# A decoder layer on one core: the norm before the last gate split into weights and sigmoid, and separate homes for the down projection's sums and one load buffer

## The chip, the cores and the metric

The kernel runs on one core of one Trainium2 chip. The metric is the device time of one execution in microseconds (us), lower is better. The core has five engines with instruction queues of their own that run in parallel and wait for each other by semaphores: TensorE (PE; its weight loads are listed as PEld), VectorE (DVE), ScalarE (ACT), GpSimd (POOL) and SyncE (SP). Each engine takes its instructions strictly in the order in which they were written to its queue, so a waiting instruction holds up all that stand behind it. SP and POOL also issue the DMA transfers.

## What is computed

One decoder layer on 512 tokens of width 1024, in float32. The parts that matter here are the last three: the down projection of the MLP, its norm, and the gated input embedding.

```
ff = (gelu(u_gate) * u_val) @ w_down            # (512, 2816) @ (2816, 1024)
x = x + rmsnorm(ff, mlp_post_norm)
e = p @ w_ple                                    # (512, 256) @ (256, 1024)
out = x + sigmoid(rmsnorm(x, ple_norm) @ w_ple_gate) * e
rmsnorm(t, g) = t * rsqrt(mean(t * t, -1) + 1e-6) * g
```

## The kernel before, in words

**Precision.** Every matrix is kept as a pair hi + lo: ACT copies the float32 source to a rounded type (`hi`, L72), DVE subtracts (`lo`, L73). `mm3` (L56 is its helper) makes one product out of three matmuls: hi*hi, hi*lo, lo*hi. A weight arrives by `chunk` (L137): a DMA into a raw buffer, then this split.

**Buffers.** SBUF is handed out by pools that open and close like a stack on each side. Raw buffers come from rings: `W["rings"]["raw"]` is `rawp` (2) + `rawb` (1), and for the first half of the down projection the pool `rx` adds 2 more, so 5. `rx` is opened after `close_qp()`, on the memory that the pool `qp` held. `qp` holds the tiles `X` and `f2h` of the up projection, from which POOL writes each pair's sums to DRAM (`dd`, L797). A raw buffer of `rx` can thus be loaded only when those DMAs have read their source.

**Up projection.** For each of 22 blocks `j`, 48 matmuls into two PSUM banks `pu`; ACT and DVE do the convolution and GELU (`conv_gelu`, L814 to L822), and after every second block `ff_sums` (L785 to L797) makes sums of token blocks.

**Down projection.** It is Strassen's scheme with seven products on 2x2 blocks, over 11 chunks `c`. The first half takes for each chunk two raw tiles of `w_down` (`r1`, 512 KB, L888; `r2`, 256 KB, L889), makes their sums and differences on DVE (L893 to L895), and runs 24 matmuls into the eight banks `M1`, `M5`, `M7`, `M6`. `drain` (L916 to L923) then combines the banks into six tiles: `U`, `V12` and `C22`, two each. In the second half every chunk needs one raw tile more (L934) and 12 matmuls (into `M1` and `M3`); then `M4` follows with 66 matmuls whose right sides were kept in SBUF as `T2`. `T2t` are two tiles of 8 x 512 elements: `T2t[0]` and three slots of `T2t[1]` hold the `T2`, and the other five slots of `T2t[1]` hold five of the six tiles out of `drain`; the sixth is `T4v`.

**Norms and gate.** `post_norm(n, ...)` (L720) takes one block of 128 tokens: squares and their sum on ACT (L725), the power -1/2 on POOL (L728), scaling by the gain on DVE (L731), the residual add into `xn` (L732), the square of `xn` on ACT (L733), the power on POOL (L102), and the scaling by that and by the gain `g_next` on DVE (L735) into `t`. `to_hT` (L738) transposes `t` by 8 matmuls with the identity into PSUM (`ptr`, L60), and ACT and DVE split it into `hT[0]` and `hT[1]` (L747, L748). At the end `hT` is allocated anew as `h3T` on the memory of `T2t`: its lo half is on `T2t[1]`. The gate is 192 matmuls into `pg`; `finish` and `last_halves` apply the sigmoid (ACT), multiply by `e`, add `xn` (DVE) and store.

**Order.** The order of each engine's queue is set by a scheduler when the program is built, which goes by its own estimate of durations, by the priorities (`hot`) and by when buffers come free. So a change of a buffer's home moves instructions on all engines. Transfers issued by `load` (L865) are tied into one order on POOL.

Of the kernel before, what the change touches and what calls it, by code (L numbers as in the profile page):

```python
# [29 lines left out]

PP_QA, PP_KVA, PP_BG, PP_W0, PP_W1, PP_W2, PP_CB = 0, 2, 3, 19, 63, 107, 151
PP_N = 195

# [4 lines left out]
def hybrid_kernel(ctx, tc, T):  # L38
# [97 lines left out]

    def chunk(src, n=1024, parts=1, dst=None):  # L137
        raw = wtile("raw" if not W["slots"] or (W["raw"] + W["lo"]) & 2 == 0 else "lo", F32)
        w = n // parts
        for i in range(parts):  # L140
            nc.sync.dma_start(raw[:, i * w:(i + 1) * w], src[:, i * w:(i + 1) * w])
        hi = dst[0] if dst else wtile("hi", F32R)
        if dst:
            lo = dst[1]
        elif W["slots"]:
            lo = W["slots"].pop(0)
            W["slots"].append(lo)
        else:
            lo = wtile("lo", F32R)
        if parts == 1:  # L150
            split(hi[:, :n], lo[:, :n], raw[:, :n])
        else:
            for i in range(parts):
                u = slice(i * w, (i + 1) * w)
                dve.tensor_copy(hi[:, u], raw[:, u])
                dve.tensor_tensor(lo[:, u], raw[:, u], f32(hi[:, u]), ALU.subtract)
        return hi, lo
# [495 lines left out]

    def loadgain(src, go=nc.sync.dma_start):
        t = res["bcp"].tile([P, D], F32, name="gain", tag="gain", bufs=2)
        go(t, src.partition_broadcast(P))
        return t
# [61 lines left out]

    def post_norm(n, ps, gp, gn):  # L720
        xn = res["xn"]
# [135 lines left out]
    close_qp()  # L857
    vp, close_vp = opened(name="vp", bufs=1, side="right")
    rx, close_rx = opened(name="rx", bufs=1, side="right")
    R2 = W["rings"]["raw"]  # L860
    W["rings"]["raw"] = R2 + [(rx, 2)]

# [41 lines left out]

    T4v = vp.tile([P, S], F32, name="T4v")
    close_rx()
    W["rings"]["raw"] = R2
    open_res()
    xn = res["xn"]
    g_post, g_next = loadgain(T["mlp_post"], load), loadgain(T["ple_norm"], load)  # L910
    for n in range(NB):
        load(xn[:, n, :], xd[n])
    parts = [T2t[1][:, i] for i in range(3, 8)] + [T4v]
    U, V12, C22 = (parts[2 * i:2 * i + 2] for i in range(3))

# [32 lines left out]
    for n in range(2):  # L948
        dve.tensor_tensor(V12[n], M3[n], V12[n], ALU.add)
        ts[n] = post_norm(n, (M["M1"][n], V12[n]), g_post, g_next)  # L950
    M4 = banks(2, "M4")
# [18 lines left out]
    for n in (2, 3):  # L970
        dve.tensor_tensor(U[n - 2], M4[n - 2], U[n - 2], ALU.add)
        ts[n] = post_norm(n, (U[n - 2], C22[n - 2]), g_post, g_next)


    for n in range(NB):
        b = slice(n * P, (n + 1) * P)
        for half in range(2):
            ps = bank(1 + 2 * (n % 2), "pe")
            w = slice(half * S, (half + 1) * S)
            for k in range(2):  # L980
                mm3(ps, ph[:, k, b], pl[:, k, b], wph[:, k, w], wpl[:, k, w], k == 0, k == 1)
            act.activation(e[:, n, w], ps, AF.Copy)
    hT = [hp.tile([P, 8, S], F32R, name=f"h3T{i}", tag=f"hT{i}") for i in range(2)]
    for n in range(NB):
        to_hT(n, ts[n], n // 2 * 2)
    cg = [chunk(T["wpg"][k]) for k in range(4)]
    wx = [qkp.tile([P, 4, 1024], F32R, name="wy" + t, tag=t) for t in ("kT", "qT")]
    cg += [chunk(T["wpg"][4 + k], dst=[t[:, k, :] for t in wx]) for k in range(4)]
    lB = fp.tile([P, 4, S], F32, name="lB", tag="fB")
# [15 lines left out]
    def last_halves(n, half):  # L1005
        g = [bank(n, "pg") for _ in range(2)]
        b = slice(n * P, (n + 1) * P)
        for i in range(2):
# [4 lines left out]
            o = otile()[:, :256]  # L1013
            act.activation(o, g[i][:, :256], AF.Sigmoid)
            dve.tensor_tensor(o, o, e[:, n, u], ALU.mult)
# [3 lines left out]
    def finish(n, half, pg, parts=1):  # L1019
        o = otile()  # L1020
        q = S // parts
        for i in range(parts):
            u = slice(i * q, (i + 1) * q)
            w = slice(half * S + i * q, half * S + (i + 1) * q)
            act.activation(o[:, u], pg[:, u], AF.Sigmoid)
            dve.tensor_tensor(o[:, u], o[:, u], e[:, n, w], ALU.mult)
            dve.tensor_tensor(o[:, u], o[:, u], xn[:, n, w], ALU.add)
            nc.sync.dma_start(T["out"][n * P:(n + 1) * P, w], o[:, u])

    pg = {(n, half): bank(1 + 2 * n, "pg") for n in (0, 1) for half in range(2)}  # L1030
    gate_mms(pg, (0, 1), (0, 1))
# [18 lines left out]
def layouts(i):  # L1050
# [19 lines left out]
    pp = np.concatenate([col(i["q_a_norm"][0]), col(i["kv_a_norm"][0]),  # L1070
                         col(i["b_gate"][0]), cw[0], cw[1], cw[2], cb], 1)
    q, k = np.arange(P)[:, None], np.arange(P)[None, :]
# [28 lines left out]
        "mlp_post": f(np.asarray(i["mlp_post_norm"])[0]),  # L1101
        "ple_norm": f(np.asarray(i["ple_norm"])[0]),
        "cst": f(cst),
# [33 lines left out]
```

## Time and profile before

| | us |
|---|---|
| median of 3 runs (lowest, highest) | 761.18 (760.98, 762.81) |
| the profiled execution | 759.25 |
| its span, first to last instruction | 757.5 |
| PE busy | 731.1 (97%) |
| DVE busy | 534.3 (71%) |
| ACT busy | 362.3 (48%) |
| mean granted clock of TensorE | 0.985 |

The median is 1.93 us above the profiled execution, and this is 1.75 us above its span. Busy time of PE counts a matmul until its modelled end, so "busy" is no measure of speed: when the clock is granted at half, PE is just as busy and does half the work. Idle time of an engine matters only where nothing else was due on the one that ends last; a wait is put down to the releaser that came last.

### The profile page before, as it was taken

Reading aid. Unit: us, or ns where it says so; the run is one execution under the profiler, and the core shown is the slowest. Engines: PE = TensorE matmul, PEld = TensorE weight load, DVE = VectorE, ACT = ScalarE, POOL = GpSimd, SP = SyncE. Lnnn points to the kernel's source line nnn. Section 1 sums busy time; section 2 is a strip of 40 time slices with the busy share of each in tenths; the row PEclk is TensorE's granted clock in tenths of the full one; section 3 lists DMA queues with packets and bytes.
Section 4 is the critical chain, followed back from the end, with each engine's and each line's share of the span. In section 5 each row is a group of like instructions: output and inputs, shape, how many; then the busy total and the mean of one; then the engine's idle time right before and its main releaser. Section 6 shows DMA issues by size and latency. Waiting matters only on the chain.

```text
span 757.5 us, 9555 instructions
## 1 busy us (share of the span) xinstructions
PE 731.1 (97%) x3496; PEld 605.7 (80%) x3496; DVE 534.3 (71%) x939; ACT 362.3 (48%) x634; POOL 84.3 (11%) x100
## 2 busy tenths in 40 slices
PE   9999999999999999999999999999985999999797
PEld 8988877778888778898888888888874888787686
DVE  6568788986775493849767676767657866789632
ACT  5843677755444243638444544444323443377321
POOL 0104023000000150200000000000000223001100
PEclk9999999999999999999999999999995999999999
DMA  8612221222122545514434344433314987946011
GB/s 308 244 32 63 60 84 42 66 74 71 42 84 84 192 141 167 172 52 141 144 133 138 140 138 141 133 125 110 133 55 155 318 263 238 353 132 195 0 57 56
DMA packets 30959, 99.90 MB, mean 132 GB/s; under 512 B 4128, under 2 KB 5408, under 8 KB 30912
## 3 DMA queue, kind: packets, MB, share of 16 engines
q1 hardware_dynamic: 25248, 76.75, 30.8%
q0 software_dynamic: 5664, 22.55, 8.2%
q8 instruction: 27, 0.44, 0.2%
q14 instruction: 20, 0.16, 0.1%
HBM read 85.98 MB, written 12.85 MB: 130 GB/s over the span
## 4 chain that ended last, share of the span: by engine, by line
PE 61%; issue 26%; DVE 7%; DMA 3%; ACT 1%; POOL 1%; SPq 0%; POOLq 0%; DVEq 0%
PE M L56 12%; PE psg L56 11%; PE pg L56 6%; PE yo L56 6%; PE pu L56 4%; PE puh L56 3%; PE psA L56 3%; PE psba L56 3%; PE psC L56 2%; PE psB L56 2%; PE scm L56 2%; DVE wlo L73 2%; DMA wraw<-in_wd 1%; PE pb L56 1%; POOL dd L797 1%
## 5 line engine op out<-in xcount | busy, mean ns | idle before, releaser
L56 PE MATMUL pu<-hT,whi 128*128 128x512 f32 x640 | 197.1, 389 | 0.0
L72 ACT ACTIVATE whi<-wraw 128x1024 fp32r<-128x1024 f32 (+4 forms) x109 | 106.7, 980 | 182.3 <-PE pu L56 75.3
L73 DVE TENSOR_TENSOR wlo<-wraw,whi 128x1024 fp32r<-128x1024 f32 (+2 forms) x103 | 120.5, 1173 | 69.0 <-ACT whi L72 65.5
L56 PEld LDWEIGHTS pu<-hT,whi 128*128 128x128 f32 x640 | 120.1, 188 | 24.8
L56 PE MATMUL pu<-hT,wlo 128*128 128x512 f32 x320 | 124.5, 389 | 0.0
L56 PEld LDWEIGHTS pu<-hT,wlo 128*128 128x128 f32 x320 | 60.1, 188 | 12.6
L56 PE MATMUL psg<-xh,whi 128*128 128x512 f32 x128 | 51.1, 400 | 1.3 <-DVE ga L422 0.9
L56 PE MATMUL psg<-xl,whi 128*128 128x512 f32 x128 | 50.8, 397 | 0.0
L56 PE MATMUL psg<-xh,wlo 128*128 128x512 f32 x128 | 50.8, 397 | 0.0
L814 ACT ACTIVATE cv<-pu,pp 128x512 f32<-128x512 f32 x40 | 30.6, 765 | 9.1 <-PE pu L56 9.1
L815 DVE SCALAR_TENSOR_TENSOR cv<-pu,pp,cv 128x511 f32<-128x511 f32 x40 | 29.8, 745 | 4.7 <-ACT cv L814 4.7
L72 ACT ACTIVATE whi<-T 128x512 fp32r<-128x512 f32 (+1 forms) x33 | 24.4, 766 | 17.4 <-PE M L56 12.2
L56 PE MATMUL M<-whi,ffxh 128*128 128x512 f32 x64 | 22.4, 439 | 9.3 <-ACT whi L72 9.3
L816 DVE SCALAR_TENSOR_TENSOR cv<-pu,pp,cv 128x510 f32<-128x510 f32 x40 | 29.9, 747 | 1.1
L817 ACT ACTIVATE cv<-cv 128x512 f32<-128x512 f32 x22 | 13.9, 632 | 33.6 <-DVE cv L816 33.6
L797 POOL DMA_DIRECT2D dd<-f2h x11 | 6.0, 546 | 214.9 <-ACT f2h L794 214.9
L670 POOL TENSOR_TENSOR gx<-gx,ga 128x512 f32<-128x512 f32 x8 | 14.8, 1870 | 133.3 <-DVE gx L669 133.3
L56 PEld LDWEIGHTS psg<-xh,whi 128*128 128x128 f32 x128 | 24.0, 188 | 7.0 <-DVE ga L422 1.1
L73 DVE TENSOR_TENSOR wlo<-T,whi 128x512 fp32r<-128x512 f32 (+1 forms) x33 | 27.3, 862 | 1.0 <-ACT whi L72 0.9
L56 PEld LDWEIGHTS psg<-xl,whi 128*128 128x128 f32 x128 | 24.1, 188 | 4.9 <-issue 0.2
L56 PEld LDWEIGHTS psg<-xh,wlo 128*128 128x128 f32 x128 | 24.1, 188 | 4.8
L56 PEld LDWEIGHTS M<-whi,ffxh 128*128 128x128 f32 x64 | 13.4, 214 | 13.3 <-ACT whi L72 10.5
(314 smaller groups left out, 1652.6 us busy)
## 6 DMA issues: line engine op xcount, KB each, us to landing
wraw<-in_wup SPq DMA_DIRECT2D x44, 512.0 KB, 3.4
wraw<-in_wd SPq DMA_DIRECT2D x22, 512.0 KB, 4.7
wraw<-in_wg SPq DMA_DIRECT2D x16, 512.0 KB, 3.4
dd<-f2h POOLq DMA_DIRECT2D x11, 384.0 KB, 3.0
dd<-X POOLq DMA_DIRECT2D x11, 384.0 KB, 2.6
wraw<-in_wo SPq DMA_DIRECT2D x8, 512.0 KB, 3.8
wraw<-in_wpg SPq DMA_DIRECT2D x8, 512.0 KB, 3.7
wraw<-in_wd SPq DMA_DIRECT2D x11, 256.0 KB, 4.7
```

The lines of the kernel that those rows point to most:

```text
L56: pe.chain(out, nc.tensor.matmul(out, *a, **k))
L72: act.activation(hi, src, AF.Copy)
L73: dve.tensor_tensor(lo, src, f32(hi), ALU.subtract)
L670: pool.tensor_tensor(ta, ta, ga[:, m, :], ALU.add)
L797: pool.dma_start(dd[c][:, i], f32(v))
L814: act.activation(c, u, AF.Identity, scale=w2, bias=cb)
L815: dve.scalar_tensor_tensor(c[:, 1:], u[:, :S - 1], w1, c[:, 1:], ALU.mult, ALU.add)
L816: dve.scalar_tensor_tensor(c[:, 2:], u[:, :S - 2], w0, c[:, 2:], ALU.mult, ALU.add)
L817: act.activation(cs[0], cs[0], AF.Gelu_apprx_tanh)
```

## The change

1. The gain `ple_norm` is no longer multiplied into the tokens. It is a column of `pp` (8 columns more), and the gate weight is split with it: ACT copies `raw * g`, DVE forms `raw * g - hi` in one instruction (`chunk` with `g`). The broadcast load of `ple_norm` goes.
2. The factor rsqrt(...) of the norm is applied by the sigmoid, as its `scale`. `post_norm` without `gn` returns the factor, and L735 is not issued for these four blocks. The transposes read `xn` itself, so they wait for the residual add and not for the square, the power and the scaling.
3. `U` gets a tile of its own in `vp` (4 KB per partition, where `T4v` had 2), `C22` one of the three `t` tiles of the pool `ck`; only `V12` stays in `T2t[1]`.
4. `rx` is opened before `qp`, so nothing else is on its memory from the end of the attention's norm on. It has one buffer instead of two, and the ring of the first half is 4 instead of 5.
5. The PSUM banks of `pe`, `ptr` and `pg` at the end are other ones.

```diff
-    def chunk(src, n=1024, parts=1, dst=None):
+    def chunk(src, n=1024, parts=1, dst=None, g=None):
...
-        if parts == 1:
+        if g is not None:
+            act.activation(hi, raw, AF.Copy, scale=g)
+            dve.scalar_tensor_tensor(lo, raw, g, f32(hi), ALU.mult, ALU.subtract)
+        elif parts == 1:
...
-    def post_norm(n, ps, gp, gn):
+    def post_norm(n, ps, gp, gn=None):
...
         rsqrt(r2, s2, 1.0 / D, 1)
+        if gn is None:
+            return r2
         dve.scalar_tensor_tensor(t, xn[:, n, :], r2, gn, ALU.mult, ALU.mult)
...
     close_res()
+    rx, close_rx = opened(name="rx", bufs=1, side="right")
     qp, close_qp = opened(name="qp", bufs=1, side="right")
...
     close_qp()
-    vp, close_vp = opened(name="vp", bufs=1, side="right")
-    rx, close_rx = opened(name="rx", bufs=1, side="right")
     R2 = W["rings"]["raw"]
-    W["rings"]["raw"] = R2 + [(rx, 2)]
+    W["rings"]["raw"] = R2 + [(rx, 1)]
...
-    T4v = vp.tile([P, S], F32, name="T4v")
     close_rx()
     W["rings"]["raw"] = R2
+    vp, close_vp = opened(name="vp", bufs=1, side="right")
...
-    g_post, g_next = loadgain(T["mlp_post"], load), loadgain(T["ple_norm"], load)
+    g_post = loadgain(T["mlp_post"], load, 1)
...
-    parts = [T2t[1][:, i] for i in range(3, 8)] + [T4v]
-    U, V12, C22 = (parts[2 * i:2 * i + 2] for i in range(3))
+    Ut = vp.tile([P, 2, S], F32, name="U")
+    C22t = ck.tile([P, 2, S], F32, name="C22", tag="t", bufs=3)
+    U, C22 = ([t[:, b] for b in range(2)] for t in (Ut, C22t))
+    V12 = [T2t[1][:, 4 + b] for b in range(2)]
...
-            ps = bank(1 + 2 * (n % 2), "pe")
+            ps = bank(3 * (n % 2), "pe")
...
-        to_hT(n, ts[n], n // 2 * 2)
-    cg = [chunk(T["wpg"][k]) for k in range(4)]
+        to_hT(n, xn[:, n, :], 1 + n // 2)
+    gp = lambda k: pp[:, PP_PLE + k:PP_PLE + k + 1]
+    cg = [chunk(T["wpg"][k], g=gp(k)) for k in range(4)]
...
-            act.activation(o, g[i][:, :256], AF.Sigmoid)
+            act.activation(o, g[i][:, :256], AF.Sigmoid, scale=ts[n])
...
-            act.activation(o[:, u], pg[:, u], AF.Sigmoid)
+            act.activation(o[:, u], pg[:, u], AF.Sigmoid, scale=ts[n])
...
-    pg = {(n, half): bank(1 + 2 * n, "pg") for n in (0, 1) for half in range(2)}
+    pg = {(n, half): bank(3 * n, "pg") for n in (0, 1) for half in range(2)}
```

The scheduler moves instructions at two places. Up to the end of the up projection the queues are the same, except that one load has moved forward on SP. Numbers behind a name tell the buffers apart.

**SP, from the last weight of the up projection on, before.** Chunk 0 of the down projection is `wraw_4975` (r1) and `wraw_4976` (r2); chunk 1 is `wraw_5018` and `wraw_5019`; chunk 2 is `wraw_5061` and `wraw_5062`.

```order
L141 DMA wraw_4882<-in_wup 128x1024
L889 DMA wraw_5019<-in_wd 128x512
L888 DMA wraw_4975<-in_wd 128x1024
L888 DMA wraw_5061<-in_wd 128x1024
L889 DMA wraw_4976<-in_wd 128x512
L888 DMA wraw_5018<-in_wd 128x1024
L889 DMA wraw_5062<-in_wd 128x512
```

And now, at the same place; r2 of chunk 1 (`wraw_5016`) stands 38 rows further ahead, among the up projection's weights.

```order
L141 DMA wraw_4885<-in_wup 128x1024
L892 DMA wraw_4972<-in_wd 128x1024
L892 DMA wraw_5015<-in_wd 128x1024
L893 DMA wraw_4973<-in_wd 128x512
L892 DMA wraw_5058<-in_wd 128x1024
L893 DMA wraw_5059<-in_wd 128x512
```

Both tiles of chunks 0 and 1 now stand directly behind the up projection's weights, ahead of any tile of chunk 2.

**DVE, from the first difference of the down projection on, before** (`cv` and `X` belong to the last block of the up projection, `T21` and `T20` are the down projection's differences).

```order
L893 TENSOR_TENSOR T21_4966<-wraw_4975 128x512
L815 SCALAR_TENSOR_TENSOR cv_4938<-pu_4889,pp_59,cv_4938 128x511
L816 SCALAR_TENSOR_TENSOR cv_4938<-pu_4889,pp_59,cv_4938 128x510
L822 TENSOR_TENSOR X_4874<-cv_4938 128x2x256
L787 TENSOR_TENSOR X_4874<-X_4874 128x256
L789 TENSOR_TENSOR X_4874<-X_4874 128x256
L790 TENSOR_TENSOR X_4874<-X_4874 128x256
L73 TENSOR_TENSOR fffB_4642<-X_4874,fffA_4641 128x1024
L795 TENSOR_TENSOR X_4874<-X_4874,f2h_4953 128x768
L894 TENSOR_TENSOR T21_4966<-wraw_4976,wraw_4975 128x512
L895 TENSOR_TENSOR T20_4965<-wraw_4976,T21_4966 128x512
L893 TENSOR_TENSOR T21_4966<-wraw_5018 128x512
```

And now:

```order
L897 TENSOR_TENSOR T21_4963<-wraw_4972 128x512
L898 TENSOR_TENSOR T21_4963<-wraw_4973,wraw_4972 128x512
L897 TENSOR_TENSOR T21_4963<-wraw_5015 128x512
L898 TENSOR_TENSOR T21_4963<-wraw_5016,wraw_5015 128x512
L899 TENSOR_TENSOR T20_4962<-wraw_4973,T21_4963 128x512
L821 SCALAR_TENSOR_TENSOR cv_4941<-pu_4892,pp_59,cv_4941 128x511
L899 TENSOR_TENSOR T20_4962<-wraw_5016,T21_4963 128x512
L73 TENSOR_TENSOR wlo_4979<-T21_4963,whi_4978 128x1024
L73 TENSOR_TENSOR wlo_5020<-wraw_5015,whi_5019 128x512
L822 SCALAR_TENSOR_TENSOR cv_4941<-pu_4892,pp_59,cv_4941 128x510
L73 TENSOR_TENSOR wlo_5022<-T21_4963,whi_5021 128x1024
L73 TENSOR_TENSOR wlo_4977<-T20_4962,whi_4976 128x512
```

The differences of the first two chunks now come first, and the up projection's last sums are spread over some 30 instructions behind them. On ACT the same: the two copies for the last `X` stood ahead of the first copy of `T21`, and stand 11 and 13 rows behind it now.

**PE, at the end of M4, before** (`pe` is the product for `e`, `ptr` a transpose, `pg` the gate).

```order
L56 MATMUL pe<-wpt,lA 128x512 x35
L60 MATMUL ptr<-ident,t 128x128 x8
L56 MATMUL pe<-wpt,lA 128x512 x12
L56 MATMUL pg<-whi,h3T_5947 128x512
L56 MATMUL pg<-wlo,h3T_5947 128x512
L56 MATMUL pg<-whi,h3T_5947 128x512
L56 MATMUL pg<-wlo,h3T_5947 128x512
L60 MATMUL ptr<-ident,t 128x128 x4
```

And now:

```order
L60 MATMUL ptr<-ident,xn 128x128 x8
L56 MATMUL pe<-wpt,lA 128x512 x30
L60 MATMUL ptr<-ident,xn 128x128 x8
L56 MATMUL pe<-wpt,lA 128x512 x18
L60 MATMUL ptr<-ident,xn 128x128 x8
L56 MATMUL pg<-whi,h3T_5942 128x512
```

Three of the four blocks are now transposed before the gate's first matmul, with the `pe` matmuls between them; before, it was one block.

## Rows read from the trace of the kernel before

**Rows 1.** The page's 40 equal slices of the span: tenths busy, or of the clock.

```profile
PE   9999999999999999999999999999985999999797
PEclk9999999999999999999999999999995999999999
```

**Rows 2.** Who waited for whom: PE's longest waits, total, times, longest one.

```profile
PE M L56 <- ACT whi L72: 9.3, 2, 7.6
PE ptr L60 <- DVE h3T L748: 4.6, 1, 4.6
```

**Rows 3.** Stretches: length; PE, PEld, DVE, ACT, POOL busy; clock, DMA share, GB/s.

```profile
564.49:590.80 26.31, 16.39 (x52) 11.91 (x50) 19.96 (x29) 9.74 (x12) 2.54 (x4) 0.68 0.46 148
590.80:640.06 49.26, 49.26 (x213) 39.88 (x212) 35.81 (x49) 20.22 (x28) 12.74 (x18) 1.00 0.83 275
687.20:753.21 66.01, 61.19 (x296) 50.31 (x294) 34.73 (x50) 24.73 (x43) 4.91 (x6) 0.97 0.21 71
```

**Rows 4.** Timeline of PE at the start of the down projection: start, length, idle before.

```profile
565.62 0.39 PE L56 MATMUL M<-whi,ffxl 128*128 128x512 f32 x1
573.65 2.93 PE L56 MATMUL M<-whi,ffxh 128*128 128x512 f32 x6 [7.63 <-ACT whi L72]
578.28 1.22 PE L56 MATMUL M<-whi,ffxh 128*128 128x512 f32 x2 [1.70 <-ACT whi L72]
580.09 0.79 PE L56 MATMUL M<-wlo,ffxh 128*128 128x512 f32 x1 [0.58 <-DVE wlo L73]
```

**Rows 5.** The chain that ended last, there: start, length, what.

```profile
570.80 2.59 DMA dd<-f2h
...
573.46 4.12 DMA wraw<-in_wd
```

**Rows 6.** Timeline of DVE and ACT there.

```profile
564.47 0.69 DVE L893 TENSOR_TENSOR T<-wraw 128x512 f32<-128x512 f32 x1 [2.87 <-PE pu L56]
...
578.81 1.22 DVE L73 TENSOR_TENSOR wlo<-T,whi 128x1024 fp32r<-128x1024 f32 x1
579.95 0.68 DVE L895 TENSOR_TENSOR T<-wraw,T 128x512 f32<-128x512 f32 x1
580.55 0.68 DVE L73 TENSOR_TENSOR wlo<-T,whi 128x512 fp32r<-128x512 f32 x1
...
564.69 0.78 ACT L814 ACTIVATE cv<-pu,pp 128x512 f32<-128x512 f32 x1 [2.37 <-PE pu L56]
...
572.54 1.58 ACT L72 ACTIVATE whi<-T 128x1024 fp32r<-128x1024 f32 x2 [2.03 <-DVE T L894]
```

**Rows 7.** Timeline of SP's queue there; a row is an issue, with its own length.

```profile
545.05 0.33 SPq L888 DMA_DIRECT2D wraw<-in_wd  x1
```

**Rows 8.** Stretches of 2 us (columns as rows 3): where the clock falls and returns.

```profile
568.00:570.00 2.00, 0.00 (x0) 0.00 (x0) 1.27 (x4) 1.28 (x2) 0.00 (x0) 0.55 0.00 0
...
584.00:586.00 2.00, 2.00 (x7) 1.55 (x6) 2.00 (x5) 0.58 (x1) 0.00 (x0) 0.68 0.16 62
...
706.00:708.00 2.00, 2.00 (x7) 1.61 (x6) 1.56 (x2) 1.63 (x3) 1.30 (x1) 0.50 0.00 0
```

**Rows 9.** A stretch with a short wait of PE (1.2 of 5 us), columns as rows 3.

```profile
275.00:280.00 5.00, 3.80 (x17) 3.14 (x18) 5.00 (x5) 2.21 (x3) 3.77 (x3) 1.00 0.32 105
```

**Rows 10.** What raw buffers did from 560 to 690 us.

```profile
DMA to landing us min/median/max: 3.2/4.6/7.5
```

**Rows 11.** Timeline of DVE, then PE, at the end of the last norm.

```profile
702.62 0.74 DVE L731 SCALAR_TENSOR_TENSOR t<-T4v,q,gain 128x512 f32<-128x512 f32 x1
...
705.25 1.08 PE L60 MATMUL ptr<-ident,t 128*128 128x128 f32 x4 [4.63 <-DVE h3T L748]
```

**Rows 12.** Groups by line and form: count, busy, mean ns, idle before.

```profile
L735 DVE SCALAR_TENSOR_TENSOR t<-xn,q,gain 128x1024 f32<-128x1024 f32 x8 | 10.2, 1282 | 2.6 <-POOL q L102 2.5
L198 ACT ACTIVATE xh<-xraw,gatt 128x512 fp32r<-128x512 f32 x7 | 4.7, 712 | 2.6 <-DMA xraw<-in_xT 2.6
L72 ACT ACTIVATE whi<-wraw 128x512 fp32r<-128x512 f32 x15 | 9.5, 630 | 27.2 <-PE M L56 17.2 <-PE pu L56 3.7 <-DMA wraw<-in_wd 3.5
```

More of the change, by code (lines that the diff above doesn't have):

```diff
@@ L28 @@
 MAGIC = 12582912.0
-PP_QA, PP_KVA, PP_BG, PP_W0, PP_W1, PP_W2, PP_CB = 0, 2, 3, 19, 63, 107, 151
-PP_N = 195
+PP_QA, PP_KVA, PP_BG, PP_W0, PP_W1, PP_W2, PP_CB, PP_PLE = 0, 2, 3, 19, 63, 107, 151, 195
+PP_N = 203
 CS_ID, CS_ONE, CS_SWA, CS_CAU, CS_INV = 0, 128, 256, 512, 1024
@@ L652, in hybrid_kernel, with loadgain @@
     p3 = [accT, accT, scT, scT, scT, ptT, ptT, pvT]
-    def loadgain(src, go=nc.sync.dma_start):
-        t = res["bcp"].tile([P, D], F32, name="gain", tag="gain", bufs=2)
+    def loadgain(src, go=nc.sync.dma_start, bufs=2):
+        t = res["bcp"].tile([P, D], F32, name="gain", tag="gain", bufs=bufs)
         go(t, src.partition_broadcast(P))
@@ L949, in hybrid_kernel @@
         dve.tensor_tensor(V12[n], M3[n], V12[n], ALU.add)
-        ts[n] = post_norm(n, (M["M1"][n], V12[n]), g_post, g_next)
+        ts[n] = post_norm(n, (M["M1"][n], V12[n]), g_post)
     M4 = banks(2, "M4")
@@ L971, in hybrid_kernel @@
         dve.tensor_tensor(U[n - 2], M4[n - 2], U[n - 2], ALU.add)
-        ts[n] = post_norm(n, (U[n - 2], C22[n - 2]), g_post, g_next)
+        ts[n] = post_norm(n, (U[n - 2], C22[n - 2]), g_post)
     for n in range(NB):
@@ L984, in hybrid_kernel @@
     for n in range(NB):
-        to_hT(n, ts[n], n // 2 * 2)
-    cg = [chunk(T["wpg"][k]) for k in range(4)]
+        to_hT(n, xn[:, n, :], 1 + n // 2)
+    gp = lambda k: pp[:, PP_PLE + k:PP_PLE + k + 1]
+    cg = [chunk(T["wpg"][k], g=gp(k)) for k in range(4)]
     wx = [qkp.tile([P, 4, 1024], F32R, name="wy" + t, tag=t) for t in ("kT", "qT")]
-    cg += [chunk(T["wpg"][4 + k], dst=[t[:, k, :] for t in wx]) for k in range(4)]
+    cg += [chunk(T["wpg"][4 + k], g=gp(4 + k), dst=[t[:, k, :] for t in wx]) for k in range(4)]
     lB = fp.tile([P, 4, S], F32, name="lB", tag="fB")
@@ L1070, in layouts @@
     pp = np.concatenate([col(i["q_a_norm"][0]), col(i["kv_a_norm"][0]),
-                         col(i["b_gate"][0]), cw[0], cw[1], cw[2], cb], 1)
+                         col(i["b_gate"][0]), cw[0], cw[1], cw[2], cb,
+                         col(i["ple_norm"][0])], 1)
     q, k = np.arange(P)[:, None], np.arange(P)[None, :]
@@ L1101, in layouts @@
         "mlp_post": f(np.asarray(i["mlp_post_norm"])[0]),
-        "ple_norm": f(np.asarray(i["ple_norm"])[0]),
         "cst": f(cst),
```

## Prediction

> **What bounds the kernel now.** The page's slices come first: PE is busy in nine tenths or more of nearly every slice, at full clock, with two dents, at slices 30 and 31 and at slice 38, and a fall of the clock to half at the first [rows 1]. The view of waits names what makes them: PE waited twice for ACT's copy of a weight, 9.3 us in all, and once for DVE's lo half of `h3T`, 4.6 us [rows 2]. Everywhere else PE is the bound, so an edit is worth something only in these two places, or where it makes PE wait anew.
>
> The first dent is the start of the down projection. Its first 50 matmuls took 26.31 us, at a mean clock of 0.68 [rows 3]. The next 214 took 49.26 us with no idle time, 0.23 us each. At that pace 50 take 11.5 us, so 14.8 us are lost there. The timeline shows how: six matmuls from 564.49 on, then three waits of 7.63, 1.70 and 0.58 us, 9.9 in all [rows 4]; the other 4.9 us are the matmuls between them at half clock. The clock falls in 568 to 570, some 2 us after PE went idle, and is back only between 584 and 586, some 5 us after PE began to run without waits at 580.09 [rows 8]. The chain of waits gives the cause of the second and third: the load of chunk 1's r1 was issued only at 573.46, right after the last `f2h` had been written to DRAM (570.80 and 2.59 us), because its buffer in `rx` is on that memory, and it landed 4.12 us later [rows 5]. The first wait is one of order: on DVE the second difference of chunk 0 stands behind eight instructions of the up projection, as the change's section shows, so ACT could start the copy that PE waits for only at 572.54 [rows 6].
>
> The second dent is the last norm. After M4, PE needed 66.01 us to its last matmul, 61.19 of them busy [rows 3]. It stood still for 4.63 us before the second block's transposes [rows 11]. They waited for DVE to empty a bank into `h3T`'s lo half, and this lies where `U` and `C22` lay, which `post_norm` read up to 702.62 and 0.74 us. From 705.25 until past 708 the clock was half [rows 8], and this cost half of 2.75 us, 1.4.
>
> **The change part by part.** First the loads. The last of the three shared raw buffers came free for an issue at 545.05 [rows 7]; the three loads that stand behind the up projection's weights are now r1 of chunk 0, r1 of chunk 1 and r2 of chunk 0, and r2 of chunk 1 has been in `rx` for long. With 7.5 us as the slowest landing [rows 10], chunks 0 and 1 are all there by 553, ahead of 564.47, when DVE makes its first difference [rows 6].
>
> Then the order, walked with the steps of rows 6: a 512 wide DVE operation takes a slot of 0.60 us, a 1024 wide one 1.14. DVE has the two differences of chunk 0 by 565.7, those of chunk 1 by 566.9, chunk 0's third by 567.5. One convolution step, a slot of 0.7 us as for the 0.74 of L731 [rows 11], and one difference bring it to 568.8; the lo half of chunk 0's T21 ends at 570.0, the raw one of chunk 1 at 570.6, and after a convolution step and 1.14 us chunk 1's T21 at 572.5, then two more by 573.7. ACT is free at 565.5 [rows 6], and its copies, 1.1 and 0.6 us (their sum is the 1.58 of rows 6), end at 566.9 (chunk 0's T21), 567.4, 568.4 and 568.9 (chunk 0's third). PE has done its first six at 565.9 and waits 1.0 us for the first copy, runs six, waits 0.6 for 568.9, runs one, waits 0.9 for the lo half at 570.0, and from there each operand is there before its turn: chunk 1's lo half at 572.5 is due at 573.9, and chunk 2's at 576, since its r1 is issued when DVE leaves the buffer at 565.7 and lands by 570 to 573. That makes 2.5 us of waits in place of 14.8: **12.3 us saved**, at full clock, which the rivals doubt. The up projection's last sums, moved behind, have no reader before the reload of the last pair, at the end of this half.
>
> The 4 buffers instead of 5: a chunk takes two and PE needs 24 x 0.23 = 5.5 us per chunk, so a buffer must come back within 11 us. DVE holds it for about 3 us (three differences and a lo half at 0.60, and their hand-overs), and the load takes 3.2 to 7.5 [rows 10]: 6.2 to 10.5. It fits, with 0.5 us left in the worst case seen, so I take nothing and keep up to 1 us for each of 9 chunks as the upper bound. Nothing below zero: the buffers only limit.
>
> The `ple_norm` load: one of 512 KB less in a stretch where PE hardly waited; nothing.
>
> The tail, in the times of before. PE ends M4 at 687.2. Then come 8 transposes (0.9 us; four at half clock took 1.08 with the modelled end [rows 11]), 30 `pe` (6.9), 8 transposes, 18 `pe` (4.1), 8 transposes, and the gate from about 700.9. Blocks 0 and 1 have their residual before M4 ends. Block 2 is due at 700.0, 12.8 us after M4; until its add DVE has two sums with M4's banks, three weights, two lo halves of `h3T`, four scalings and the add: 1.2 + 3 x 1.2 + 1.2 + 4 x 0.7 + 1.1 = 9.9 us, by rows 6, 11 and 12. 2.9 us are left for what DVE itself waits for. Block 3 is due 5 us later, for one more weight and add, 2.3. So the wait of 4.63 goes with the rest of the idle time, 66.01 - 61.19 = 4.82, and the 1.4 of clock with it. DVE loses four scalings of 1.28 and pays 1.28 in place of 1.22 for eight weights; ACT pays 0.08 more where a column scales (0.712 against 0.630 [rows 12]), eight times beside PE's work, and once in the last sigmoid on the path: 0.1. **6.1 us saved.** Should the cover of the `pe` matmuls fail, the price is the wait that remains, up to these 6.1.
>
> Sum: 12.3 + 6.1 = 18.4. The span 757.5 becomes 739.1, the profiled execution 759.25 becomes 740.9, and the median, 1.93 above it, **742.8 us**.
>
> **Rivals.** (A) The clock falls all the same. For it: three waits within 4 us, with PE at work in less than half of that time. Against it: a wait of 1.2 us within 5 left the clock at 1.00 [rows 9], and at 568 it fell after 2 us without any matmul [rows 8]. Price: half clock from about 569 to 5.3 us after the last wait, so about 5.5 us at half, 2.8 us: 745.6. The Trainium skill, "TensorE: Matmul & The Clock Gate", section "A second HAM failure mode: psum-queue depth-cycling", tells of short stops between groups of matmuls, often enough repeated, that made the clock swing between its two levels; by that rule the time would be this rival's, and no row here has such a group of short stops.
>
> (B) The ring of four: landings near 7.5 us are the rule, since reloads of the sums through POOL go on at the same time and DMA is at 0.83 of its time in this half [rows 3]. At 0.5 to 1 us per chunk it costs 4.5 to 9: 747.3 to 751.8.
>
> (C) The tail doesn't do what it says: the banks. `pe`, transposes and gate share eight, and ACT empties them in between with eight weight copies of more than 1 us in its queue. PE then waits for ACT instead of DVE. For it: PE's longest waits are for ACT's copies now [rows 2]. Against it: a bank is asked for again only after 6 us or more of other matmuls. It gives back half to all of the 6.1: 745.9 to 748.9.
>
> (D) Slower: the same ring, but with landings far above those seen. To lose 18.4 us in 9 chunks the period must be 2.0 us longer, 7.5, a turnaround of 15 us and so a landing of 12, against 7.5 at most [rows 10]. From there on the kernel is slower than before; at 14 us it would be 3 x 9 - 18.4 = 8.6 us slower, 770.
>
> **How the numbers follow.** The forecast gets 0.53, A 0.15, B 0.15, C 0.13, D 0.04. The forecast's own case reaches from 740.3 (all of the 14.8 comes back, not 12.3 of it) to 744.5 (two of the waits a microsecond longer). The range goes from 739.8 to 751, which leaves out D, the upper end of B and a little below: about 0.15 together. A change of under 0.3%, 2.3 us, can't be told from none; this needs a loss of 16 to 20 us somewhere, 0.01. Faster 0.95, slower 0.04.
>
> **What would show it.** In the timeline of PE after 564 the first wait should be about 1 us, none above 1.5, and the clock should stay at 1.00: if it doesn't, A. The matmul that stands 51st should start near 579 instead of 590.8. Between there and the end of the first half PE should have no idle time; waits for `wlo` or `whi` behind a DMA of `in_wd` would mean B or D. After M4 no wait of PE should be over 0.5 us; one for `e` or `h3T` on ACT means C. If the first wait is as long as before, the loads or DVE's order are not what I read them to be, and the prediction fails by its larger term.

## The result and the profile after

| | before | after |
|---|---|---|
| median of 4 runs each, us | 761.97 | 742.47 |
| lowest, highest | 760.98, 762.81 | 741.82, 743.23 |
| the profiled execution | 759.25 | 741.87 |
| its span | 757.5 | 740.1 |

The ratio is 0.9745, with a 95% interval of 0.9725 to 0.9765. The forecast was 742.8.

The page of after, 40 slices as in [rows 1]: PE is at nine tenths or more in all but the 1st, the 15th and the last, the two dents are gone, and the DMA engines are at their fullest in slices 33 to 35, the down projection:

```profile
PE   8999999999999989999999999999999999999997
PEclk9999999999999999999999999999999999999999
DMA  8611221112112266242433334334322798945111
```

The waits of PE from 564 us to the end, total, times and longest, in place of [rows 2]. The wait for `h3T` is gone, and those for `w_down` are small:

```profile
PE M L56 <- ACT whi L72: 1.2, 2, 0.9
PE M L56 <- DVE wlo L73: 0.6, 1, 0.6
```

The timeline of PE at the start of the down projection, in place of [rows 4]. The first `M` matmul and the three waits:

```profile
566.70 0.39 PE L56 MATMUL M<-whi,ffxh 128*128 128x512 f32 x1
...
569.11 1.67 PE L56 MATMUL M<-whi,ffxh 128*128 128x512 f32 x6 [0.89 <-ACT whi L72]
571.10 0.50 PE L56 MATMUL M<-whi,ffxh 128*128 128x512 f32 x1 [0.32 <-ACT whi L72]
572.23 0.50 PE L56 MATMUL M<-wlo,ffxh 128*128 128x512 f32 x1 [0.62 <-DVE wlo L73]
```

Three stretches, in place of [rows 3] and with its columns: the first 50 matmuls of the down projection, from there to the end of M4, and from M4 to PE's last matmul. The clock is 1.00 in all three:

```profile
566.70:580.75 14.05, 12.22 (x52) 9.23 (x50) 14.05 (x22) 6.20 (x9) 1.13 (x2) 1.00 0.49 145
580.75:676.19 95.44, 95.44 (x413) 77.37 (x412) 79.86 (x111) 48.11 (x70) 19.86 (x31) 1.00 0.77 271
676.19:735.36 59.17, 59.15 (x297) 49.49 (x295) 29.80 (x46) 25.32 (x42) 4.88 (x6) 1.00 0.24 82
```

The timeline of PE behind M4, in place of [rows 11]. Three blocks are transposed before the gate begins at 689.95, with nothing idle between them:

```profile
676.19 1.03 PE L60 MATMUL ptr<-ident,xn 128*128 128x128 f32 x8
676.98 7.25 PE L56 MATMUL pe<-wpt,lA 128*128 128x512 f32 x30
684.07 1.03 PE L60 MATMUL ptr<-ident,xn 128*128 128x128 f32 x8
684.87 4.45 PE L56 MATMUL pe<-wpt,lA 128*128 128x512 f32 x18
689.15 1.03 PE L60 MATMUL ptr<-ident,xn 128*128 128x128 f32 x8
```

By stretches the 17.4 us of the span are: 12.26 from the first 50 matmuls (26.31 to 14.05), 0.97 from there to M4's end (95.44; before, 590.80 to 687.21), 6.84 behind M4 (66.01 to 59.17), less 0.46 at the end (4.74 from the last matmul to the end of the span; 4.28 before) and 2.21 before the down projection, which began at 566.70 and not at 564.49.

### The profile page after: what moved, and what is told of

Same layout as the page of the kernel before. It is cut to its first block, busy times and chain, and to the rows that moved or that the text cites. A ratio compares the mean times of both kernels' runs of the same rounds, so it can differ in the third digit from the quotient of the medians.

```text
span 740.1 us, 9536 instructions
## 1 busy us (share of the span) xinstructions
PE 724.9 (98%) x3496; PEld 602.7 (81%) x3496; DVE 528.8 (71%) x935; ACT 362.2 (49%) x634; POOL 83.7 (11%) x99
## 4 chain that ended last, share of the span: by engine, by line
PE 90%; DVE 6%; DMA 1%; issue 1%; ACT 1%; SPq 0%; DVEq 0%; ACTq 0%
PE pu L56 29%; PE M L56 14%; PE psg L56 11%; PE yo L56 6%; PE pg L56 6%; PE puh L56 3%; PE psba L56 3%; PE psA L56 3%; PE psC L56 2%; PE psB L56 2%; PE scm L56 2%; PE pe L56 2%; PE pb L56 1%; PE pvm L56 1%; PE ptm L60 1%
## 5 line engine op out<-in xcount | busy, mean ns | idle before, releaser
L72 ACT ACTIVATE whi<-wraw 128x1024 fp32r<-128x1024 f32 (+4 forms) x105 | 102.1, 975 | 169.9 <-PE pu L56 75.6
L73 DVE TENSOR_TENSOR wlo<-wraw,whi 128x1024 fp32r<-128x1024 f32 (+2 forms) x99 | 115.7, 1172 | 64.6 <-ACT whi L72 61.2
L56 PEld LDWEIGHTS pu<-hT,wlo 128*128 128x128 f32 x320 | 60.1, 188 | 12.3
L56 PE MATMUL puh<-hT,whi 128*128 128x256 f32 x128 | 23.8, 285 | 0.1
L581 ACT ACTIVATE sm<-sm,nm 128x512 f32<-128x512 f32 (+3 forms) x32 | 17.6, 552 | 12.5 <-DVE nm L578 12.4
```

Source lines behind the costliest of these rows:

```text
L56: pe.chain(out, nc.tensor.matmul(out, *a, **k))
L72: act.activation(hi, src, AF.Copy)
L73: dve.tensor_tensor(lo, src, f32(hi), ALU.subtract)
L581: act.activation(s[:, w], s[:, w], AF.Exp, bias=nm[:, n:n + 1], accum_out=sums[:, n:n + 1])
```

## The experiments

In the table, "down" is the time from the first `M` matmul to M4's end and "tail" from there to PE's last matmul, both read from the timeline of PE in each profile; "at 640" is a wait of PE at the beginning of the second half of the down projection, between 637 and 655 us, for a lo half of `w_down` (the second one of e4 for a hi half).

| kernel | median, us | ratio to before [95%] | down | tail | at 640 |
|---|---|---|---|---|---|
| before | 761.97 to 763.01 | | 122.7 | 66.0 | 0.23 |
| after | 742.47 | 0.9745 [0.9725, 0.9765] | 109.5 | 59.2 | none |
| e1 raw home alone | 750.17 | 0.9835 [0.9804, 0.9867] | 111.9 | 65.9 | 1.70 |
| e2 tail alone | 752.76 | 0.9870 [0.9838, 0.9903] | 123.9 | 59.2 | 0.65 |
| e3 one buffer, shared | 755.13 | 0.9906 [0.9875, 0.9937] | 125.1 | 59.2 | 0.76 |
| e4 ring of three | 745.83 | 0.9770 [0.9730, 0.9809] | 114.3 | 59.2 | 1.56, 1.45 |
| e5 sums back | 742.33 | 0.9750 [0.9717, 0.9783] | 112.2 | 58.9 | 2.18 |
| e6 factor on tokens | 742.87 | 0.9744 [0.9715, 0.9773] | 110.2 | 59.3 | 0.50 |
| e7 banks back | 741.91 | 0.9733 [0.9709, 0.9757] | 110.9 | 59.2 | 1.10 |
| e8 first difference early | 738.00 | 0.9688 [0.9667, 0.9708] | 108.0 | 59.2 | 1.01 |
| e9 own scratch | 743.81 | 0.9776 [0.9738, 0.9814] | 110.4 | 60.2 | 0.44 |
| e10 ring kept | 738.79 | 0.9705 [0.9675, 0.9735] | 107.5 | 59.1 | 0.51 |
| e11 after again | 742.52 | 0.9737 [0.9710, 0.9764] | 112.4 | 59.2 | 2.71 |
| e12 first difference again | 740.25 | 0.9720 [0.9690, 0.9749] | 110.6 | 59.2 | 2.04 |

### The start of the down projection

**e1: the raw buffer's home alone**, on the kernel before.

```diff
     close_res()
+    rx, close_rx = opened(name="rx", bufs=1, side="right")
     qp, close_qp = opened(name="qp", bufs=1, side="right")
...
     close_qp()
-    vp, close_vp = opened(name="vp", bufs=1, side="right")
-    rx, close_rx = opened(name="rx", bufs=1, side="right")
...
-    W["rings"]["raw"] = R2 + [(rx, 2)]
+    W["rings"]["raw"] = R2 + [(rx, 1)]
...
     W["rings"]["raw"] = R2
+    vp, close_vp = opened(name="vp", bufs=1, side="right")
```

> The kernel before with one part of the change: rx is opened ahead of qp with one buffer, so the ring is 4 and no raw buffer shares memory with X and f2h; T4v moves behind the loop because of that. Norm, homes of the sums and banks as before. Two separate gains (my theory): the 12.3 us at the start of the down projection come, the 6.1 of the tail don't: about 762.0 - 12.3 = 749.7 us, 748 to 751; first wait of PE there about 1 us, the 51st matmul 14 us after the first; the wait of some 4.6 us for h3T's lo half is still there. Rival (the two gains are one, the start of the down projection only moved what the tail waits for): under 746 or over 754.

Measured: 750.17 us. The three waits at the start are 0.89, 0.34 and 0.62 us, as after; the tail is as long as before, with the wait of 4.63 us at the same place. So this edit carries the larger term by itself.

**e2: everything but that**, on the changed kernel.

```diff
-    rx, close_rx = opened(name="rx", bufs=1, side="right")
     qp, close_qp = opened(name="qp", bufs=1, side="right")
...
     close_qp()
+    vp, close_vp = opened(name="vp", bufs=1, side="right")
+    rx, close_rx = opened(name="rx", bufs=1, side="right")
...
-    W["rings"]["raw"] = R2 + [(rx, 1)]
+    W["rings"]["raw"] = R2 + [(rx, 2)]
...
-    vp, close_vp = opened(name="vp", bufs=1, side="right")
```

> The changed kernel with rx as before: opened after qp's close, two buffers, ring of 5. Norm split, own homes of the sums and new banks stay. My theory: the start of the down projection is as before, three waits of about 10 us in all and half clock, the tail without waits: 762.0 - 6.1 to 6.8 = 755.5 us, 754 to 757. Rival (the homes of the sums or the order they bring also move the start): under 752.

Measured: 752.76 us, 1.2 below the lower end. The stretches are as expected: down 123.9 with a longest wait of 7.6 us and half clock, as before; tail 59.2. Its profiled execution is 753.56, 5.7 below that of before, and the stretches explain it. The medians say 10.3. All 24 runs of the kernel before that were timed beside the experiments are above its profiled execution (759.48 to 764.29 against 759.25), and the median of e2 is 0.8 below its own. So I add up stretches, not medians: against the 763.01 of the kernel before, timed beside them, the medians of e1 and e2 gain 12.8 and 10.3, more together than the 19.5 of the whole change.

**e3: one buffer, but on `qp`'s memory**, on the changed kernel.

```diff
-    rx, close_rx = opened(name="rx", bufs=1, side="right")
     qp, close_qp = opened(name="qp", bufs=1, side="right")
...
     close_qp()
+    rx, close_rx = opened(name="rx", bufs=1, side="right")
```

> The changed kernel with rx's one buffer back on qp's memory: opened after qp's close, ring of 4 as after. Theory H (the home decides, as my prediction reads it: a load that must wait for the last f2h's write is late): its load comes only after the writes of X and f2h, and PE waits 5 us or more at half clock: 750 to 757 us. Rival O (the order decides, that is which load falls to that buffer: with 4 buffers it is the second raw tile of chunk 1, no longer the first, and the matmuls of chunk 2 are put ahead of it): both differences of chunk 0 are made at once, the late load hides behind the matmuls of chunks 0 and 2, and the time is that of the changed kernel within 2 us: 741 to 744.5.

Measured: 755.13 us, theory H. The rows, of PE, DVE, SP and POOL in e3's timeline:

```profile
566.10 1.91 PE L56 MATMUL M<-whi,ffxh 128*128 128x512 f32 x7 [0.89 <-ACT whi L72]
586.76 2.93 PE L56 MATMUL M<-whi,ffxh 128*128 128x512 f32 x6 [12.48 <-ACT whi L72]
...
584.92 0.69 DVE L898 TENSOR_TENSOR T<-wraw 128x512 f32<-128x512 f32 x1 [4.85 <-DMA wraw<-in_wd]
...
580.60 0.33 SPq L893 DMA_DIRECT2D wraw<-in_wd  x1
...
579.16 0.56 POOL L802 DMA_DIRECT2D dd<-X  x1 [1.58 <-DVE X L800]
```

The last `X` of the up projection is written to DRAM from 579.16 on, the load of chunk 1's r2 into the shared buffer is issued at 580.60, and DVE has it at 584.92; PE waits 12.48 us and runs on at half clock. The order was better than before (chunk 0 ran through with waits of 0.89 and 0.47), and this did not help: with a small ring, whatever stands in the late buffer is needed within two chunks. The home is the cause, and one late buffer is enough.

**e4: no `rx` at all**, a ring of three on the changed kernel.

```diff
-    rx, close_rx = opened(name="rx", bufs=1, side="right")
...
-    W["rings"]["raw"] = R2 + [(rx, 1)]
+    W["rings"]["raw"] = R2 + []
```

> The changed kernel without rx: a ring of 3 raw buffers for the first half of the down projection, all of them on memory of their own. A chunk takes two, so a buffer must be back within 1.5 chunks, 8.3 us. By the working of the prediction a turnaround is 6.2 to 10.5 us, 8.1 with the landing of 5.1 us that is the median after: nothing lost at the median, up to 1.5 us per chunk at the worst: 742.5 to 757, I take 747, with waits of PE for ACT's or DVE's halves of w_down behind a DMA. Rival (the home is all and the count of buffers never matters): 742.5 within 1 us, no wait after the first chunk.

Measured: 745.83 us (741.53 to 746.88). In the first half the smaller ring shows as two waits, 0.19 and 0.81 us; 3.0 us more are at the beginning of the second half, where every kernel here has a ring of three except e10. So the step from four to three costs about 1 us of waits in the first half, at the lower end of my bounds. That fits the usual landing (after, from 560 to 690 us: 4.5 us in the median of all loads into raw buffers, with 2.9 and 7.8 as ends) better than the slowest. At the start e4 gains as much: it has only the first of the three waits, 0.89 us, and its first 50 matmuls take 12.92 us, where after has 14.05. Why was not looked into.

### The tail

**e5: the sums where they were** (`U`, `V12`, `C22` in `T2t[1]` and `T4v`), on the changed kernel.

```diff
-    Ut = vp.tile([P, 2, S], F32, name="U")
-    C22t = ck.tile([P, 2, S], F32, name="C22", tag="t", bufs=3)
-    U, C22 = ([t[:, b] for b in range(2)] for t in (Ut, C22t))
-    V12 = [T2t[1][:, 4 + b] for b in range(2)]
+    T4v = vp.tile([P, S], F32, name="T4v")
+    parts = [T2t[1][:, i] for i in range(3, 8)] + [T4v]
+    U, V12, C22 = (parts[2 * i:2 * i + 2] for i in range(3))
```

> The changed kernel with the homes of the sums as before (U, C22 and V12 in T2t[1] and T4v); norm split, banks and raw ring as after. Theory H (the tail's wait was one of memory: h3T's lo half could not be written before post_norm had read U and C22): PE waits again for h3T's lo half on DVE. PE has work for 13 us after the end of M4, and the first lo half comes 12.5 to 16 us after it, so the wait is 0.5 to 4.5 us, with some half clock behind: 743.5 to 748.5, I take 746.5 us. Rival N (the wait belonged to the norm's longer chain, square, power and scaling, which the residual no longer goes through): as the changed kernel, 742.5 within 1 us.

Measured: 742.33 us, tail 58.9. Theory H fell: the shared home by itself, with tokens that are not scaled, costs nothing. DVE's last read of the sums and the first lo half of `h3T`, in e5:

```profile
687.35 0.74 DVE L734 SCALAR_TENSOR_TENSOR t<-T4v,q,gain 128x512 f32<-128x512 f32 x1
688.01 1.28 DVE L152 SCALAR_TENSOR_TENSOR wyqT<-wraw,pp,wykT 128x1024 fp32r<-128x1024 f32 x1
689.21 1.28 DVE L753 TENSOR_TENSOR h3T<-ptr,h3T 128x512 fp32r<-128x512 f32 x2
```

Block 3's sums are read 10.3 us behind M4's end (677.05), where the kernel before did it at 15.4 [rows 11], and PE still has `pe` matmuls.

**e6: the factor on the tokens again**, on the changed kernel. The sigmoids have no `scale`; the scratch of blocks 2 and 3 lies where the out tiles lie, as in e9 below, since `C22` has one of the three `t` tiles.

```diff
         if gn is None:
-            return r2
+            dve.tensor_scalar(t, xn[:, n, :], r2, None, ALU.mult)
+            return t
...
-        to_hT(n, xn[:, n, :], 1 + n // 2)
+        to_hT(n, ts[n], 1 + n // 2)
```

> The changed kernel, but the rsqrt factor is multiplied into the tokens ahead of the transposes again (one DVE operation for each block, the gain stays in the weights), and the sigmoids have no scale; homes, banks and ring as after. The scratch of blocks 2 and 3 lies where the out tiles lie, since C22 has one of the three t tiles. By my theory both halves of the tail's edit are needed: block 2 has its residual 10.8 us after M4's end and its transposes are due at 12.8; square, power and scaling add 4 to 5 us, so PE waits 2 to 3 us for block 2 and hardly for block 3: 744.5 to 747 us. Rival (the homes alone made the gain): 742.5 within 1 us.

Measured: 742.87 us, tail 59.3, no wait. My theory that both halves are needed fell too: the scaled blocks 2 and 3 are transposed only from 698.33 on, 22.6 us behind M4's end, and until then PE has the `pe` matmuls and the gate's of blocks 0 and 1. But this kernel has moved the scratch as well, and that led to the next theory. The rows of e1, whose tail is that of before, PE then ACT then DVE:

```profile
684.25 1.03 PE L60 MATMUL ptr<-ident,t 128*128 128x128 f32 x8
694.08 1.08 PE L60 MATMUL ptr<-ident,t 128*128 128x128 f32 x4 [4.63 <-DVE h3T L748]
...
686.84 0.64 ACT L725 ACTIVATE t<-T 128x512 f32<-128x512 f32 x1
...
691.45 0.75 DVE L731 SCALAR_TENSOR_TENSOR t<-T4v,q,gain 128x512 f32<-128x512 f32 x1
```

ACT's squares of block 3 write a `t` tile. There are three, and block 0 holds one until its transposes, at 684.25. So the squares start at 686.84, DVE reads the sums up to 692.2, and only then can the lo half of block 0 be written, into memory that the sums occupied. As I read these rows, the wait needs all three: three tiles, scaled tokens held in them, and the shared home. e9 tests the first; e5 had taken away the second.

**e9: e1 and a scratch of its own** for blocks 2 and 3, nothing else.

```diff
...
+    lB = fp.tile([P, 6, S], F32, name="lB", tag="fB")
+    tt = [lB[:, i:i + 2].rearrange("p a t -> p (a t)") for i in (4, 2)]
     for n in (2, 3):
...
-        ts[n] = post_norm(n, (U[n - 2], C22[n - 2]), g_post, g_next)
+        ts[n] = post_norm(n, (U[n - 2], C22[n - 2]), g_post, g_next, t=tt[n - 2])
...
-    lB = fp.tile([P, 4, S], F32, name="lB", tag="fB")
```

> The kernel with only the raw buffer's home changed (first experiment), and one edit more: the scratch tile t of blocks 2 and 3 in the last norm lies where the out tiles lie, and not in the three tiles of ck. Gain, factor, homes of the sums and banks are those of the kernel before. Theory T (block 3's squares write a t tile that block 0 holds until it is transposed, and only after that can the sums be read and h3T's lo half be written: the wait needs the held tile as well as the shared home): no wait for h3T after M4, the tail 59 to 60 us long and not 66: 750.2 - 6.8 = 743.4 us, 742 to 745. Theory H (the shared home of sums and lo half alone): the wait of some 4.6 us stays, 749 to 751.

Measured: 743.81 us, tail 60.2; theory T. What is left of the wait, in e9's timeline of PE:

```profile
688.48 0.66 PE L60 MATMUL ptr<-ident,t 128*128 128x128 f32 x4 [0.36 <-DVE h3T L749]
```

So the held tile can be taken away in two ways, by not scaling the tokens (e5) or by another scratch (e9). That the home alone, with scaled tokens in the three tiles, would do it too was not tried: `C22` would then need a fourth place. So the shared home as the third condition is argued, not shown.

**e7: the banks of before**, on the changed kernel.

```diff
-            ps = bank(3 * (n % 2), "pe")
+            ps = bank(1 + 2 * (n % 2), "pe")
...
-        to_hT(n, xn[:, n, :], 1 + n // 2)
+        to_hT(n, xn[:, n, :], n // 2 * 2)
...
-    pg = {(n, half): bank(3 * n, "pg") for n in (0, 1) for half in range(2)}
+    pg = {(n, half): bank(1 + 2 * n, "pg") for n in (0, 1) for half in range(2)}
```

> The changed kernel with the PSUM banks of pe, ptr and pg as before. My prediction took the new banks for worth nothing by themselves: 742.5 within 1 us, no wait after M4. Rival (they keep the transposes off banks that ACT empties late): PE waits for e or h3T on ACT for 1 us or more in the tail: 743.5 to 746.

Measured: 741.91 us, tail 59.2, no wait behind M4. The banks are worth nothing by themselves.

### A version that is faster

**e8: the first difference early**, on the changed kernel.

```diff
-        t13 = T13[c % 2]
+        t13 = T13[c % 2] if c else ck.tile([P, D], F32, name="t13", tag="t", bufs=3)
```

> The changed kernel with one more edit: the differences of chunk 0 are written to a tile t of ck, and not to the memory of hT, which the up projection's last matmul still reads. In the changed kernel the first difference starts only when that matmul is done, and PE waits 0.89, 0.32 and 0.62 us in the first chunk. If that home causes them, DVE makes the two differences ahead of a convolution step, and 1 to 1.8 us go: 740.7 to 741.5 us, waits of PE in the first chunk under 0.6 us in all. Rival (the tile is missing to the convolution, or the order moves so that other operands are late): 742.5 us or more.

Measured: 738.00 us, 2.7 below the lower end. DVE's first difference in the timeline of after, then in that of e8, then the first 14.05 us of e8's down projection as a stretch:

```profile
566.67 0.69 DVE L897 TENSOR_TENSOR T<-wraw 128x512 f32<-128x512 f32 x1 [2.87 <-PE pu L56]
```

```profile
559.06 0.68 DVE L897 TENSOR_TENSOR t<-wraw 128x512 f32<-128x512 f32 x1
```

```profile
566.29:580.34 14.05, 14.05 (x63) 11.64 (x62) 14.04 (x23) 7.65 (x11) 2.86 (x4) 1.00 0.54 164
```

In after, DVE was idle for 2.87 us and waited for the last matmul of the up projection, since the differences lie on the memory of `hT`. In e8 they are there 7 us ahead, no wait stands at the start, and 63 matmuls run where after has 52. The 51st starts 11.33 us after the first, and in after 14.05: 2.7 us.

**e12: the same, beside the changed kernel (e11) on one chip.**

> The changed kernel as it is, beside the others of this call. 742.5 within 1 us; clock at full in the down projection and in the tail; one fall of the clock near 108 or near 276 with about 1.7 us of work lost, as in seven of ten profiles so far.

> The kernel with the early first difference once more, to set it beside the changed kernel on the same chip: its first 50 matmuls of the down projection are 1.8 us shorter, so 740.7 us if nothing else differs; 738 us as in its first run if the runs of the changed kernel were the ones with chance losses.

Measured: 742.52 us (740.20 to 744.21) and 740.25 (738.31 to 743.84). So the edit gives 2.3 us here, near the 2.7 of the stretch; the 4.5 between the first median of e8 and the 742.47 of the changed kernel are partly chance, and the intervals of e11 and e12 overlap. Both kernels pay a wait at 640 here. Of e11, the timeline of PE and DVE there, and a stretch around it:

```profile
644.48 0.50 PE L56 MATMUL M<-wlo,ffkT 128*128 128x512 f32 x1 [2.71 <-DVE wlo L73]
...
638.00 0.69 DVE L943 TENSOR_TENSOR T<-wraw,T 128x512 f32<-128x512 f32 x1 [2.79 <-DMA wraw<-in_wd]
```

```profile
640.00:644.00 4.00, 1.77 (x8) 1.13 (x6) 3.19 (x5) 1.53 (x2) 0.00 (x0) 1.00 1.00 410
```

DVE waited for a load of `w_down` while the DMA engines were busy for 0.92 of the time (634 to 638 us; 1.00 in the stretch shown): from 631.4 on, POOL issues the gain and the four blocks of the residual, 2.5 MB, beside them. That these are what delays it is argued from the rows; no run took them away.

**e10: e8 with the fourth raw buffer kept through the second half**, the sums where they were (as e5) to make room for it.

```diff
-    close_rx()
-    W["rings"]["raw"] = R2
...
     close_vp()
+    close_rx()
```

> The kernel with the early first difference (738.0 us), and the fourth raw buffer kept through the second half of the down projection; for its memory the sums' homes are those of before (T2t[1] and T4v), which cost nothing by the experiment on them. In four profiles with a fast start PE waits 1.0 to 2.2 us at about 640 for a lo half behind a load of w_down, where the ring is three. If the turnaround of three buffers is the cause, that wait goes: 736 to 737.5 us. Rival (the transfers as a whole are the limit there, with the DMA share at 0.96): the wait stays, 738 to 739.

Measured: 738.79 us (737.62 to 742.21). The median lies in the rival's range. The wait at 640 is 0.51 us; the others with a ring of three have 0 to 2.7 there, so one profile doesn't settle whether buffers or transfers are the limit. e10 is 3.7 us below the changed kernel timed beside it (e11), with intervals that overlap by a little, and its profile has the shortest span of all, 736.8, though its clock fell twice on the way (below). It is the version I would keep; e8 can't be told from it.

## Why the prediction was right, and where it wasn't

**First 50 matmuls: right.** Forecast were waits of 1.0, 0.6 and 0.9 us and 12.3 saved; it was 0.89, 0.32 and 0.62, and 12.26. The sum came nearer than its parts: the waits were 0.7 us shorter in all, and PE was busy for 12.22 us with these matmuls where 11.5 were reckoned. Chunks 0 and 1 were there, the order was the one walked through, and the cause, a buffer on `qp`'s memory, holds by e1 and e3. What the walk did not ask is why DVE begins at 564.47 [rows 6]: not the loads but the memory of `hT` holds it, and e8 got another 2.7 us there.

**Clock, rival A: out.** Seven profiles (after, e1, e5, e6, e7, e9, e11) have these three waits within 4.4 us of PE, and the granted clock stays at 1.00 at that place in all seven. The Trainium skill, "TensorE: Matmul & The Clock Gate", section "A second HAM failure mode: psum-queue depth-cycling", tells of short stops between groups of matmuls that made the clock swing; three of them, once, did not do it here.

**Ring of four: right for the first half, and a term was missing for the second.** From 574 to 637 no kernel with four buffers of their own has a wait of PE over 0.3 us. The wait at 640 stands in the second half, where the ring was three before and after. It was 0.23 us before, and in the nine profiles with the fast start and this ring (after, e1, e5 to e9, e11, e12) it is 0 to 2.7, 1.3 in the mean. I read it as a part of the gain that is given back: counted from its first matmul, PE now comes to the second half some 12 us earlier, while the reload of the residual and the loads of `w_down` fill the DMA engines. The profile of after happens to have none of it. The prediction's sum should have had about 1 us here.

**Tail: the size right, the mechanism half right.** Forecast 6.1, measured 6.84 (7.1 with the one `pe` matmul that stood ahead of M4's end before). The idle time of 4.8 us went. The clock's 1.4 holds. Before, two of the stretches around the wait were (columns as [rows 3]; the one between them is in [rows 8]):

```profile
704.00:706.00 2.00, 0.75 (x5) 0.78 (x5) 2.00 (x5) 0.00 (x0) 0.16 (x1) 0.69 0.01 4
708.00:710.00 2.00, 2.00 (x10) 1.66 (x9) 1.28 (x3) 0.08 (x1) 0.55 (x1) 0.96 0.00 0
```

The means 0.69, 0.50 and 0.96 make 1.24, 2.00 and 0.16 us at half clock. In the first stretch PE was busy for only 0.75 us, so about 2.9 us of its work ran at half clock, which cost 1.5. Some 0.8 us of the 7.1 remain. Most of that is in the pace of the gate's 512 wide matmuls at full clock: thirty of them took 7.01 us before (from 721.93 on) and 6.86 after (from 705.14 on), and there are some 160. The cause of that is open. But the step "they waited for DVE to empty a bank into `h3T`'s lo half, and this lies where `U` and `C22` lay" named one condition where more are needed: I did not ask why block 3's sums were read so late, and e5 and e9 show that the `t` tile held by block 0 decided it. And what covers blocks 2 and 3 was more than I reckoned: in e6 the gate's first matmuls do it.

**ACT and DVE pay what was said.** DVE's lo halves of the gate weight took 1.28 us, the copies without a gain 1.22. On ACT a scale from a column costs about 0.09 us, as the groups of after show (weight copy with and without, sigmoid; the sigmoid was 0.599 before), and the last sigmoid 0.47 against 0.38, the forecast 0.1:

```profile
L72 ACT ACTIVATE whi<-wraw 128x1024 fp32r<-128x1024 f32 x85 | 89.7, 1059 | 147.8 <-PE pu L56 71.9 <-PE psg L56 17.7 <-DMA wraw<-in_wd 11.2
L151 ACT ACTIVATE whi<-wraw,pp 128x1024 fp32r<-128x1024 f32 x4 | 4.6, 1149 | 0.3 <-PE M L56 0.3
L1032 ACT ACTIVATE lB<-pg,q 128x512 f32<-128x512 f32 x7 | 4.5, 690 | 13.6 <-PE pg L56 13.5
```

**Rivals B, C and D** didn't come: no wait behind a load in the first half, none for the banks (e7).

**What no term was made for.** The forecast span was 739.1 and it is 740.1. Behind the start of the down projection 19.6 us were gained against the 18.4 of the sum; 2.2 us went ahead of it, where PE has the same matmuls in the same order. They are chance: some 1.0 us from later landings of the first weights, and 1.6 from one fall of the clock near 276 us (last section), less 0.3 later on; over the 14 profiles the down projection begins at 563.68 to 566.70 us. And the step "the median, 1.93 above it" took a chance as fixed: here the median is 0.6 above the profiled execution. The span 1.0 too short and the step 1.3 too long left the forecast 0.3 off. That closeness is luck, and so is the profile of after without a wait at 640.

## What to carry to other kernels

A wait on an allocated buffer has two questions, not one: whose memory is it, and who holds a tile that this owner needs first; giving either of them a place of its own may be enough, and the cheapest is worth finding by an experiment that undoes one part at a time. After an early stall is gone, look at the next place where transfers are dense: PE comes there earlier than its loads do. And before a profiled execution stands for a median, look for events in it, or missing in it, that come by chance.

## What was not expected of the hardware

**After the same short waits the clock falls in some profiles and not in others, and a fall has a price.** Two waits of PE, 1.1 and 0.4 us near 107 and 0.4 and 1.4 us near 276, are in every kernel here, since that part is the same in all. Behind the first the clock fell in 6 of 14 profiles (e2, e4, e5, e7, e10, e11), behind the second in 4 (after, e6, e8, e10). Before, e1, e3, e9 and e12 have neither. The waits themselves don't tell them apart: the first, of 1.1 us, is 1.07 to 1.16 us long in the profiles with a fall behind it and 1.06 to 1.13 in the others, the one of 1.4 us is 1.40 to 1.42 in all. What decides is not shown here. Stretches of 2 us of after, columns as [rows 3], then of e12 behind its wait at 640:

```profile
276.00:278.00 2.00, 0.77 (x2) 0.68 (x3) 2.00 (x2) 1.58 (x2) 2.00 (x2) 0.84 0.00 0
278.00:280.00 2.00, 2.00 (x6) 1.52 (x6) 2.00 (x3) 0.63 (x1) 0.77 (x2) 0.50 0.72 262
280.00:282.00 2.00, 2.00 (x9) 1.59 (x8) 2.00 (x2) 0.23 (x1) 1.74 (x1) 0.81 0.19 25
```

```profile
640.00:642.00 2.00, 2.00 (x7) 1.61 (x8) 2.00 (x3) 0.00 (x0) 0.00 (x0) 0.73 0.98 346
642.00:644.00 2.00, 2.00 (x6) 1.55 (x5) 0.86 (x2) 0.14 (x1) 0.00 (x0) 0.50 0.87 305
644.00:646.00 2.00, 2.00 (x9) 1.60 (x9) 1.52 (x2) 1.59 (x2) 0.00 (x0) 0.92 0.91 334
```

Each of these falls takes 1.7 us of full clock: 2 x (0.16 + 0.50 + 0.19) = 1.70 and 2 x (0.27 + 0.50 + 0.08) = 1.70, and the falls near 107 give 1.70 to 1.72 in the same way. The prediction's [rows 9], where such a wait left the clock alone, is one throw of this, so that row was weaker evidence against rival A than I took it for; and by these falls rival A's price of 2.8 us looks too high, though no run shows a fall behind its three waits. The falls explain only a part of the 2 to 5 us by which runs of one kernel differ: two runs of e11 whose mean clock is 1.000 took 742.52 and 740.20 us. What the rest is stays open.
